# Sums of weight blocks in a seven-product matrix multiplication: two of four per head as VectorE additions, two as accumulating transfers, and the first rotary embeddings placed inside and behind head 0

## The chip, the core and the metric

The kernel runs on one core of a Trainium2 chip. The metric is the device time of one execution in microseconds, the median over several executions. A core has a matrix engine (TensorE, PE in the profile, with its weight loads as PEld), three engines for element-wise work (VectorE is DVE, ScalarE is ACT, GpSimd is POOL) and queues that start transfers: SP's hardware queue for plain loads, and POOL's software queue, the one used here for transfers that add to what lies in the target. Each engine works through its own instructions strictly in order, so an instruction that waits holds up all those behind it on its engine.

## The reference, cut to what matters

Two layers on a sequence of 512 rows with model width 1024. Layer 0 is a retention layer with four heads, layer 1 a forgetting attention with sixteen. The change lies in layer 0, in the projection from the modulated input `h` (512 x 1024) to queries, keys, values and gates:

```python
def _retention(h, positions, w_in, w_out):
    b, s, _ = h.shape
    n = s // CHUNK
    q, k, v, g = jnp.split(h @ w_in, [RET_DK, 2 * RET_DK, 2 * RET_DK + RET_DV], axis=-1)
    q = _rope(q.astype(jnp.float32).reshape(b, s, RET_HEADS, RET_HK), positions) * (RET_HK ** -0.5)
    k = _rope(k.astype(jnp.float32).reshape(b, s, RET_HEADS, RET_HK), positions)
...
    o = _layer_norm(_from_chunks(o)).reshape(b, s, RET_DV)
    return (o.astype(h.dtype) * jax.nn.silu(g)) @ w_out
```

For one head, values and gates together are `h @ [Wv | Wg]`, a product of 512 x 1024 by 1024 x 1024.

## The kernel before

**Precision.** Weights and activations are float32. Each matrix is split into a high and a low part of type fp32r (`split`: ACT casts the high part, DVE subtracts it to get the low part), and a product is three matrix instructions: high by high, high by low, low by high (`mm3`). Of a weight block, the loaded copy is `raw` (128 x 1024), its parts are `wh` (ACT) and `wl` (DVE).

**Seven products in place of eight.** `values_gates` computes a head's values and gates by the Strassen-Winograd form. The weight [Wv | Wg] is cut into four blocks: the upper and lower half of Wv (V1, V2) and of Wg (G1, G2), each loaded as two `raw` buffers of 512 KB. `h` is cut the same way, and sums of its quarters are prepared once (`forms[1]` to `forms[4]`, tiles `sf`). The products run in this order, each of 24 matrix instructions, in two halves of the inner dimension:

1. x = h11 by V1
2. y = h12 by V2
3. v = form 1 by (V1 + G1)
4. v += form 4 by G2
5. x += form 2 by (V1 + G1 + G2)
6. x += form 3 by (G1 + G2)
7. x += h22 by (V1 + G1 + G2 + V2)

Products 3, 5 and 7 use the buffers of V1 (`first`), to which one more block is added each time. Product 4 adds onto the banks of product 3, and products 5 to 7 onto those of product 1, so results that are needed as they are get copied out of PSUM first (`keep`, ACT, tile `u`): u5 between products 3 and 4, u2 between products 5 and 6. Between products 6 and 7, DVE subtracts x from u5 (`put_g(1, ...)`, tile `big`), and product 7 may write x only after that.

**The four sums before.** All four are accumulating transfers (`plus`): POOL issues a transfer of the block from DRAM that is added to the `raw` buffer in SBUF, two for a sum, eight for a head, 32 in all. Such a transfer can start only when the previous split of that buffer has been read (`wh` by ACT, `wl` by DVE), and the next split waits until it has landed.

**What sets the order.** The program is written as a list of tasks with priorities; `Sched.order` plays it through with assumed costs and buffer counts and so fixes, ahead of the run, the order of instructions on each engine. The assumed time of flight of an accumulating transfer comes from `t.bytes`, which `cost` multiplies by 2; at 360 KB per us and with two constants (0.6 and 1.4 us) this makes 4.9 us for 512 KB. `s.at(x)` shifts the priority of what is created inside it. Buffers `raw` (8), `wh` (4), `wl` (4) and `ck` share 14 places (N_B).

**Around it.** The first queries and keys (q of head 0, k of head 0, q of head 1) are computed in the start phase, copied out of PSUM (`kept`, tiles `rt`), and rotated later by `rope`: six DVE operations of 128 x 512, and four splits. All three ropes are created ahead of head 0 with a priority 25 us later (LATE). Heads 1 to 3 are merged with the retention of the head before (`merge`), whose matrix instructions (tile `r`) also fill gaps. The modulation weights (`in_mod_w`) are loaded along the way and multiplied into `macc` on DVE.

Of the kernel before, what the change touches and what calls it, by code (L numbers as in the profile page):

```python
# [10 lines left out]
ALU = mybir.AluOpType  # L11
# [6 lines left out]
D = 1024  # L18
# [16 lines left out]

ORD = "m0:2 q0:0 k0:0 m2:2 q1:0 m4:2 q0:1 k0:1 m6:2 q1:1"

DIRECT = 4

SUMS = -22.0  # L40

TRIG, DIFF = -12.0, 0.0

KEEP, LATE = -4.0, 25.0

GO = -6.0

# [128 lines left out]
class Sched:  # L176
# [63 lines left out]
    def cost(self, t, op, args, kw, ins, outs):  # L240

        n = max([v.words() for v in outs], default=0)
        if op == "dma_start":
            v = (ins + outs)[0]
            t.bytes = 4 * v.words() * (v.part[1] - v.part[0])
            if not outs:
                t.bytes = 4 * ins[0].words() * (ins[0].part[1] - ins[0].part[0])
            if "accum_op" in kw:
                t.bytes *= 2
            return {"POOL": 1.02, "SP": 0.06, "ACT": 0.1}[t.eng]  # L250
        if t.eng == "PE":
            if op == "transpose":
                t.cols = 256
                return 0.109
            m = args[2].words()
            t.cols = m if args[2].dtype == F32R else 4 * m
            if m < 64:
                return 0.213
            return max(0.109, 0.002 + m / 2260.0) if args[2].dtype == F32R else max(0.109, m / 600.0)
        ptr = sum(isinstance(kw.get(k), View) for k in ("scale", "bias", "scalar", "scalar1"))  # L260
        if t.eng == "ACT":
            if op == "activation" and args[2] in TABLES:
                t.table = TABLES[args[2]]
            sb = ins[0].buf.kind not in PSUM_KINDS
            return 0.052 + n / 1200.0 + 0.093 * (ptr + ("accum_out" in kw)) + 0.042 * sb
        if t.eng == "POOL":
            return 0.1 + n / (1050.0 if op == "tensor_scalar" else 450.0)
        n = max([n] + [v.words() for v in ins])
        psum = any(v.buf.kind in PSUM_KINDS for v in ins + outs)
        fast = op in ("tensor_scalar", "tensor_copy") and not psum  # L270
        return 0.069 + 0.061 * ptr + n / (1920.0 if fast else 960.0)
# [227 lines left out]
def run(gen):  # L499
    for _ in gen:  # L500
        pass
# [18 lines left out]
def trunk(tc, x, c, positions, mod_w, mod_b, norm_g, ret_w_in, ret_w_out, fox_w_in, fox_b_f,  # L520
# [6 lines left out]
    with ExitStack() as es:  # L527
# [6 lines left out]
        s = Sched(tc, KINDS, {"C": (N_C, slots), "B": (N_B, slots), "G": (4, slots), "T": (24, tiny), "Z": (8, psp)})  # L534
        V, A, G, T, SY = s.vector, s.scalar, s.gpsimd, s.tensor, s.sync
# [115 lines left out]
        class MItem:  # L651


            def __init__(self, layer, cols, rows, fin, prev):
                self.layer, self.cols, self.rows, self.fin, self.prev = layer, cols, rows, fin, prev
                self.n = sum(n for _, n in cols)
                self.direct = layer == 0 and cols[0][0] == 0 and rows[-1] < DIRECT

            def load(self):
                r = s.buf("raw", 1024)  # L660
# [110 lines left out]
        def rows2(src, col, i):  # L771
            return src[:, 2 * i:2 * i + 2, col:col + 512]

        def w_s(h):


            return [Block(rows2(wi0, col, i)) for col, lo in ((vcol(h), 0), (vcol(h), 2), (gcol(h), 2), (gcol(h), 0))
                    for i in (lo, lo + 1)]

        def w_b(src, col):  # L780
# [8 lines left out]
        def vcol(h):  # L789
            return 2048 + h * 512  # L790

        def gcol(h):
            return 4096 + h * 512
# [174 lines left out]
        def quarter(i, j):  # L968

            c = slice(256 * i, 256 * i + 256)  # L970
            return [(h[:, c], l[:, c]) for h, l in hT[4 * j:4 * j + 4]]
# [75 lines left out]
        def values_gates(h):  # L1047

            vc, gc = vcol(h), gcol(h)

            def heads(raw):

                def f(i):
                    hh, ll = s.buf("wh", 1024, F32R), s.buf("wl", 1024, F32R)
                    split(raw[i], hh, ll)
                    return [(hh[:, k * 512:k * 512 + 512], ll[:, k * 512:k * 512 + 512]) for k in range(2)]
                return f

            def whole(n):
                return [R(("vg", h, n), i) for i in range(2)]

            def plus(raw, col, lo):
                with s.at(SUMS):
                    for i in range(2):
                        G.dma_start(raw[i].rearrange("p (k n) -> p k n", k=2, n=512), rows2(wi0, col, lo + i),
                                    accum_op=ALU.add)
                return heads(raw)

            def product(banks, a, w, new):
                for kp in range(2):
                    with s.at(PROC):
                        ws = w(kp)
                    for tl in range(2):
                        if new and kp == 0:
                            banks.append(pt_())
                        ts = slice(tl * P, tl * P + P)
                        for k in range(2):
                            hh, ll = a()[2 * kp + k]  # L1080
                            mm3(banks[tl], hh[:, ts], ll[:, ts], *ws[k], new and kp + k == 0, kp == 1 and k == 1,
                                skip_group_check=True)
                            yield 0.683

            def keep(banks):
                us = [s.buf("u") for _ in range(2)]
                for u, b in zip(us, banks):
                    A.copy(u, b)
                return us

            put_v, put_g = values_out(h), gates_out(h)
            x, y, v = [], [], []
            first = whole(0)
            yield from product(x, lambda: quarter(0, 0), heads(first), True)
            u1 = keep(x)
            yield from product(y, lambda: quarter(0, 1), heads(whole(1)), True)
            put_v(0, y, u1)
            yield from product(v, lambda: forms[1], plus(first, gc, 0), True)
            u5 = keep(v)
            yield from product(v, lambda: forms[4], heads(whole(2)), False)  # L1100
            yield from product(x, lambda: forms[2], plus(first, gc, 2), False)
            u2 = keep(x)
            put_g(0, v, u2)
            yield from product(x, lambda: forms[3], plus(whole(3), gc, 2), False)
            put_g(1, u5, x)
            yield from product(x, lambda: quarter(1, 1), plus(first, vc, 2), False)
            put_v(1, x, None)
# [70 lines left out]
        kept = []  # L1178
        for b in start_banks:
            kept.append(s.buf("rt"))  # L1180
            with s.at(KEEP):
                A.copy(kept[-1], b)
        with s.at(LATE):
            for i, key in enumerate((("q", 0), ("k", 0), ("q", 1))):
                rope(key, kept[2 * i], kept[2 * i + 1])

        def head(h):
            if h > 1:
# [23 lines left out]
        mask = const("mask", [P])  # L1212
        gain = const("gain", [2])

        run(head(0))
        small_operands()
        for h in range(1, RH):
            merge(head(h), retention(h - 1), R0, B0, s)

# [428 lines left out]
```

## Time and profile before

| what | us |
|---|---|
| median of three runs | 751.24 (748.67 to 754.83) |
| the profiled execution, its own time | 749.46 |
| span of the profiled execution, first to last instruction | 747.7 |

The profiled execution lies 1.78 us under the median. The span is 1.76 us shorter than that execution's time. In the profile nearly all instructions carry one line of a helper, so groups are told apart by tile names: `wl<-raw,wh` is the DVE half of a weight split, `wh<-raw` the ACT half, `u<-p` a copy out of PSUM, `macc<-raw,...` the modulation sums, `p<-wh,sf` and `p<-wh,act` are matrix instructions of the seven products. In a timeline row, the bracket at the end gives how long the engine had been idle before this instruction, and what it waited for.

### The profile page before, as it was taken

Reading aid. Unit: us, or ns where it says so; the run is one execution under the profiler, and the core shown is the slowest. Engines: PE = TensorE matmul, PEld = TensorE weight load, DVE = VectorE, ACT = ScalarE, POOL = GpSimd, SP = SyncE. Lnnn points to the kernel's source line nnn. Section 1 sums busy time; section 2 is a strip of 40 time slices with the busy share of each in tenths; the row PEclk is TensorE's granted clock in tenths of the full one; section 3 lists DMA queues with packets and bytes.
Section 4 is the critical chain, followed back from the end, with each engine's and each line's share of the span. In section 5 each row is a group of like instructions: output and inputs, shape, how many; then the busy total and the mean of one; then the engine's idle time right before and its main releaser. Section 6 shows DMA issues by size and latency. Waiting matters only on the chain.

```text
span 747.7 us, 9994 instructions
## 1 busy us (share of the span) xinstructions
PE 711.4 (95%) x3386; PEld 583.0 (78%) x3386; DVE 586.9 (78%) x1289; ACT 395.8 (53%) x733; POOL 114.4 (15%) x135
## 2 busy tenths in 40 slices
PE   7999989989997999999999999889999999999995
PEld 6777868767886888788888887668887778888884
DVE  5889987769866878798753677868698889899925
ACT  6567563535254534464322453448585677778612
POOL 1002101110121012100000101142214223120011
PEclk9999999999999999999999999999999999999998
DMA  8996948975598649935343407446435344446302
GB/s 282 349 310 143 227 134 215 240 202 189 128 205 225 229 113 203 262 125 186 113 138 102 160 37 233 136 139 157 126 90 147 95 128 118 120 125 192 118 1 112
DMA packets 78434, 122.51 MB, mean 164 GB/s; under 512 B 6712, under 2 KB 35632, under 8 KB 78384
## 3 DMA queue, kind: packets, MB, share of 16 engines
q1 hardware_dynamic: 66320, 98.78, 40.7%
q0 software_dynamic: 12064, 23.10, 17.0%
q8 instruction: 26, 0.43, 0.2%
q14 instruction: 24, 0.20, 0.1%
HBM read 113.42 MB, written 4.25 MB: 157 GB/s over the span
## 4 chain that ended last, share of the span: by engine, by line
PE 42%; DVE 7%; issue 5%; ACT 2%; POOL 1%; DMA 1%; POOLq 0%; ACTq 0%; DVEq 0%
PE a L440 18%; PE p L440 16%; PE r L440 8%; DVE t L440 3%; DVE macc L440 1%; DVE wl L440 1%; DVE st L440 1%; ACT st L440 1%; DMA ck<-cum_dram 1%; POOL ck L440 1%; DVE z L440 0%; DVE lg L440 0%; POOL qn L440 0%; ACT tm L440 0%; DVE ph L440 0%
## 5 line engine op out<-in xcount | busy, mean ns | idle before, releaser
L440 DVE TENSOR_TENSOR wl<-raw,wh 128x1024 fp32r<-128x1024 f32 x120 | 146.3, 1225 | 37.3 <-ACT wh L440 32.3
L440 ACT CAST wh<-raw 128x1024 fp32r<-128x1024 f32 x120 | 125.0, 1053 | 84.3 <-PE p L440 19.7
L440 PE MATMUL p<-wh,big 128*128 128x512 f32 x384 | 136.2, 402 | 0.0
L440 PE MATMUL p<-wh,sf 128*128 128x512 f32 x256 | 82.6, 399 | 7.4 <-ACT u L440 7.4
L440 PEld LDWEIGHTS p<-wh,big 128*128 128x128 f32 x384 | 71.9, 188 | 13.2 <-issue 0.2
L440 POOL DMA_DIRECT2D raw<-in_ret_w_in x32 | 38.9, 1263 | 267.7 <-DVE wl L440 167.9
L440 PE MATMUL p<-wl,big 128*128 128x512 f32 x192 | 76.6, 399 | 0.0
L440 PE MATMUL p<-wh,act 128*128 128x512 f32 x192 | 63.8, 402 | 5.4 <-DVE big L440 5.4
L440 DVE SCALAR_TENSOR_TENSOR macc<-raw,csilu,macc 128x512 f32<-128x512 f32 x80 | 60.6, 757 | 4.8 <-DMA raw<-in_mod_w 3.8
L440 PEld LDWEIGHTS p<-wh,sf 128*128 128x128 f32 x256 | 48.8, 191 | 19.8 <-ACT u L440 9.7
L440 PE MATMUL a<-wh,go 128*128 128x512 f32 x192 | 62.0, 393 | 0.0
L440 PE MATMUL p<-act,wh 128*128 128x512 f32 x160 | 53.2, 393 | 0.0
L440 PE MATMUL p<-wl,sf 128*128 128x512 f32 x128 | 51.1, 399 | 1.0 <-DVE wl L440 1.0
L440 PE MATMUL p<-big,wh 128*128 128x512 f32 x128 | 48.0, 424 | 0.0
L440 PEld LDWEIGHTS p<-wh,act 128*128 128x128 f32 x192 | 36.6, 192 | 13.4 <-DVE big L440 6.0
L440 ACT ACTIVATE lg<-lg,t 128x128 f32<-128x128 f32 (+1 forms) x64 | 36.3, 567 | 16.2 <-DVE t L440 14.6
L440 PEld LDWEIGHTS a<-wh,go 128*128 128x128 f32 x192 | 36.1, 188 | 7.2
L440 PEld LDWEIGHTS p<-wl,big 128*128 128x128 f32 x192 | 36.2, 188 | 6.0
L440 PE MATMUL r<-act,sh 128*128 128x512 f32 x120 | 40.3, 391 | 0.0
L440 PE MATMUL p<-wl,act 128*128 128x512 f32 x96 | 38.7, 403 | 0.7 <-DVE wl L440 0.7
L440 PE MATMUL a<-wl,go 128*128 128x512 f32 x96 | 37.5, 391 | 0.0
L440 DVE TENSOR_TENSOR ph<-r,ph 128x512 fp32r<-128x512 f32 (+2 forms) x64 | 30.7, 485 | 5.4 <-ACT ph L440 5.0
(183 smaller groups left out, 1499.0 us busy)
## 6 DMA issues: line engine op xcount, KB each, us to landing
raw<-in_ret_w_in SPq DMA_DIRECT2D x48, 512.0 KB, 6.1
raw<-in_mod_w SPq DMA_DIRECT2D x64, 256.0 KB, 6.7
raw<-in_ret_w_in POOLq DMA_DIRECT2D x32, 512.0 KB, 7.6
raw<-in_fox_w_in SPq DMA_DIRECT2D x32, 512.0 KB, 3.9
raw<-in_mod_w SPq DMA_DIRECT2D x16, 512.0 KB, 6.5
raw<-in_ret_w_out SPq DMA_DIRECT2D x16, 512.0 KB, 4.4
ck<-cum_dram SPq DMA_DIRECT2D x16, 448.0 KB, 4.6
x<-in_x SPq DMA_DIRECT2D x16, 256.0 KB, 5.2
```

The lines of the kernel that those rows point to most:

```text
L440: getattr(eng, op)(*[real(v) for v in args], **{k: real(v) for k, v in kw.items()})
```

## The change

Two of the four sums become DVE additions. G1 and G2 are now loaded as blocks of their own (`block(2)`, `block(3)`); `sum2` adds G1 to V1's buffer before product 3 and G2 before product 5, on DVE, in place, 128 x 1024, just ahead of the split. The accumulating transfers that stay are G2 onto G1's buffer (product 6, `third`) and V2 onto V1's buffer (product 7). The number of loads through SP stays at eight per head; the list of blocks `w_s` now has G1 ahead of G2, since G1 is needed first.

The ropes move: q and k of head 0 are created after 24 steps of head 0 (a step is three matrix instructions, 24 steps are three products), q of head 1 after head 0, each with a priority of 4 us later in place of 25. The planner's `t.bytes` for an accumulating transfer is multiplied by 4 in place of 2, which makes its assumed flight 7.8 us. `DIRECT` becomes a tuple; its first entry is the old value and the others are 0, so the same items are direct as before.

```diff
-DIRECT = 4
+DIRECT = (4, 0, 0, 0)
...
-KEEP, LATE = -4.0, 25.0
+KEEP, LATE = -4.0, 4.0
+
+ROPE_AT = 24
...
             if "accum_op" in kw:
-                t.bytes *= 2
+                t.bytes *= 4
...
-                self.direct = layer == 0 and cols[0][0] == 0 and rows[-1] < DIRECT
+                self.direct = layer == 0 and cols[0][0] < D and rows[-1] < DIRECT[cols[0][0] // 256]
...
-            return [Block(rows2(wi0, col, i)) for col, lo in ((vcol(h), 0), (vcol(h), 2), (gcol(h), 2), (gcol(h), 0))
+            return [Block(rows2(wi0, col, i)) for col, lo in ((vcol(h), 0), (vcol(h), 2), (gcol(h), 0), (gcol(h), 2))
                     for i in (lo, lo + 1)]
...
-            first = whole(0)
+            def sum2(raw, other):
+
+                def f(i):
+                    V.tensor_tensor(out=raw[i], in0=raw[i], in1=other()[i], op=ALU.add)
+                    return heads(raw)(i)
+                return f
+
+            kept = {}
+
+            def block(n):
+                if n not in kept:
+                    kept[n] = whole(n)
+                return kept[n]
+
+            first = block(0)
...
-            yield from product(y, lambda: quarter(0, 1), heads(whole(1)), True)
+            yield from product(y, lambda: quarter(0, 1), heads(block(1)), True)
             put_v(0, y, u1)
-            yield from product(v, lambda: forms[1], plus(first, gc, 0), True)
+            yield from product(v, lambda: forms[1], sum2(first, lambda: block(2)), True)
+            third = plus(block(2), gc, 2)
             u5 = keep(v)
-            yield from product(v, lambda: forms[4], heads(whole(2)), False)
-            yield from product(x, lambda: forms[2], plus(first, gc, 2), False)
+            yield from product(v, lambda: forms[4], heads(block(3)), False)
+            yield from product(x, lambda: forms[2], sum2(first, lambda: block(3)), False)
             u2 = keep(x)
             put_g(0, v, u2)
-            yield from product(x, lambda: forms[3], plus(whole(3), gc, 2), False)
+            yield from product(x, lambda: forms[3], third, False)
             put_g(1, u5, x)
             yield from product(x, lambda: quarter(1, 1), plus(first, vc, 2), False)
...
-        with s.at(LATE):
-            for i, key in enumerate((("q", 0), ("k", 0), ("q", 1))):
+        def start_rope(i, key, late):
+            with s.at(late):
                 rope(key, kept[2 * i], kept[2 * i + 1])
...
-        run(head(0))
+        steps = head(0)
+        for _ in range(ROPE_AT):
+            next(steps)
+        for i, key in enumerate((("q", 0), ("k", 0))):
+            start_rope(i, key, LATE)
+        run(steps)
         small_operands()
+        start_rope(2, ("q", 1), LATE)
```

How the order of instructions moves is shown at three places. A number behind a name is that buffer's own; the two programs number buffers differently.

The first place is DVE in head 0 just ahead of product 2. `rt` are ropes, `sf` and `sx` the sums of quarters of `h`, `raw_512` is V2's first buffer, and in the changed program `raw_495` and `raw_506` are V1, `raw_535` and `raw_549` G1. Before:

```order
L440 TENSOR_TENSOR sx_727<-x_613,sx_727 128x256
L440 TENSOR_TENSOR rt_740<-rt_672,trig_725 128x512
L440 TENSOR_TENSOR rt_746<-rt_672,trig_707 128x512
L440 TENSOR_TENSOR rt_672<-rt_689,trig_707 128x512
L440 TENSOR_TENSOR wl_757<-raw_512,wh_744 128x1024
```

After:

```order
L442 TENSOR_TENSOR sx_731<-sx_721,x_451 128x256
L442 TENSOR_TENSOR raw_495<-raw_495,raw_535 128x1024
L442 TENSOR_TENSOR sx_731<-x_612,sx_731 128x256
L442 TENSOR_TENSOR raw_506<-raw_506,raw_549 128x1024
L442 TENSOR_TENSOR wl_760<-raw_512,wh_744 128x1024
```

Three rope operations have left the place ahead of product 2's first split, and two additions for product 3 stand there; one `sf` that stood behind that split (`sf_161`) also stands ahead of it now, some rows earlier (`sf_144`).

The second place is DVE at the end of head 0, around the hand-over from product 6 to product 7. `raw_495` and `raw_506` are V1's buffers with all blocks added, product 7's weights; the last two `big` rows of each list are the ones that product 7 must wait for. Before:

```order
L440 TENSOR_TENSOR wl_1021<-raw_495,wh_997 128x1024
L440 TENSOR_TENSOR act_1029<-rt_908,act_1017 128x512
L440 TENSOR_TENSOR big_1038<-p_826,u_992 128x512
L440 TENSOR_TENSOR act_1044<-rt_934,act_1033 128x512
L440 TENSOR_TENSOR big_1038<-p_838,u_1009 128x512
L440 TENSOR_TENSOR wl_1055<-raw_506,wh_1040 128x1024
L440 SCALAR_TENSOR_TENSOR act_1064<-vr_841,t_853,act_1048 128x512
L440 TENSOR_TENSOR big_1038<-u_863,p_710 128x512
L440 TENSOR_TENSOR big_1038<-u_881,p_722 128x512
```

After:

```order
L442 TENSOR_TENSOR wl_1001<-raw_495,wh_966 128x1024
L442 TENSOR_TENSOR act_1008<-rt_943,act_997 128x512
L442 TENSOR_TENSOR big_1014<-p_822,u_960 128x512
L442 TENSOR_TENSOR act_1022<-rt_962,act_1010 128x512
L442 TENSOR_TENSOR big_1014<-p_834,u_975 128x512
L442 TENSOR_TENSOR big_1014<-u_862,p_710 128x512
L442 TENSOR_TENSOR big_1014<-u_872,p_719 128x512
L442 TENSOR_TENSOR sf_1052<-r_1016,dec_805 128x512
L442 TENSOR_TENSOR sf_1059<-r_1027,dec_805 128x384
L442 TENSOR_TENSOR rt_1063<-rt_736,trig_723 128x512
L442 TENSOR_TENSOR wl_1069<-raw_506,wh_1055 128x1024
```

The split of product 7's second half (`wl_1055`, `wl_1069`) stood ahead of the two `big` rows and stands four rows behind them now; the rope of q of head 1 (`rt_1063` is its first row) begins here, where it ended before.

The third place is ACT in head 1 between products 5 and 7. `u` are the copies that product 6 waits for, `raw_988` before and `raw_950` after is V1's first buffer with all blocks added. Before:

```order
L440 CAST wh_1533<-raw_1307 128x1024
L440 CAST wh_1553<-raw_988 128x1024
L440 COPY u_1565<-p_1291 128x512
L440 COPY u_1577<-p_1303 128x512
L440 ACTIVATE big_1570<-big_1570 128x512 x2
L440 CAST wh_1593<-raw_1002 128x1024
```

After:

```order
L442 CAST wh_1530<-raw_1277 128x1024
L442 COPY u_1559<-p_1283 128x512
L442 COPY u_1572<-p_1298 128x512
L442 ACTIVATE big_1564<-big_1564 128x512 x2
L442 CAST wh_1588<-raw_950 128x1024
L442 ACTIVATE big_1564<-big_1564 128x512 x2
L442 CAST wh_1636<-raw_987 128x1024
```

The cast that needs the transfer of product 7's first half stood ahead of the two copies and stands behind them now.

## The prediction

> **What bounds the kernel now.** I read the page's busy times first, then its costly groups and transfers, then windows of the heads stage, then the timeline of PE for its stalls, and from each stall back to the engine that released it. From the page:
>
> ```profile
> span 747.7 us, 9994 instructions
> PE 711.4 (95%) x3386; PEld 583.0 (78%) x3386; DVE 586.9 (78%) x1289; ACT 395.8 (53%) x733; POOL 114.4 (15%) x135
> ...
> raw<-in_mod_w SPq DMA_DIRECT2D x64, 256.0 KB, 6.7
> ...
> raw<-in_ret_w_in POOLq DMA_DIRECT2D x32, 512.0 KB, 7.6
> ```
>
> PE is busy 95% of the span, so the number of matrix instructions sets the time, and the change alters none of them. Only PE's idle time and its clock can move. A transfer that adds 512 KB takes 7.6 us from issue to landing. The change touches the four heads, 62 to 345 us. In the windows, the columns are window, length, then busy time of PE, PEld, DVE, ACT, POOL, the granted clock of PE, the share of the transfer engines, GB/s:
>
> ```profile
> 62.00:345.00 283.00, 268.52 (x1216) 220.26 (x1215) 232.47 (x437) 141.40 (x223) 37.61 (x31) 0.99 0.74 188
> 60.00:96.00 36.00, 35.27 (x156) 28.54 (x156) 35.93 (x57) 23.96 (x36) 8.54 (x7) 1.00 0.94 208
> 104.00:108.00 4.00, 4.00 (x13) 3.14 (x12) 4.00 (x6) 2.70 (x4) 0.00 (x0) 0.60 0.00 0
> 172.00:176.00 4.00, 4.00 (x20) 3.30 (x19) 3.93 (x7) 2.34 (x5) 0.00 (x0) 1.00 0.18 52
> 228.00:232.00 4.00, 2.54 (x7) 2.04 (x8) 3.87 (x5) 2.90 (x4) 0.53 (x1) 0.76 0.75 242
> 232.00:236.00 4.00, 4.00 (x16) 3.15 (x15) 2.23 (x3) 1.49 (x2) 1.91 (x2) 0.81 0.64 94
> ```
>
> In the heads PE idles 283.00 − 268.52 = 14.5 us, and DVE 50.5. The lowered clock costs (1 − 0.60) × 4 = 1.6 us at 104 to 108, and 0.24 × 2.54 + 0.19 × 4 = 1.4 us at 228 to 236. So the most that the change can gain is 14.5 + 1.6 + 1.4 = 17.5 us. PE's stalls there, in its timeline, add up to the same 14.5:
>
> ```profile
> 69.11 0.50 PE L440 MATMUL p<-wl,act 128*128 128x512 f32 x1 [0.73 <-DVE wl L440]
> ...
> 102.38 0.50 PE L440 MATMUL p<-wh,act 128*128 128x512 f32 x1 [2.74 <-DVE big L440]
> ...
> 145.79 0.50 PE L440 MATMUL p<-wh,sf 128*128 128x512 f32 x1 [0.88 <-ACT u L440]
> ...
> 155.81 0.50 PE L440 MATMUL p<-wl,sf 128*128 128x512 f32 x1 [0.96 <-DVE wl L440]
> ...
> 159.99 0.50 PE L440 MATMUL p<-wh,sf 128*128 128x512 f32 x1 [1.40 <-ACT u L440]
> ...
> 169.72 0.50 PE L440 MATMUL p<-wh,act 128*128 128x512 f32 x1 [2.62 <-DVE big L440]
> ...
> 229.46 0.50 PE L440 MATMUL p<-wh,sf 128*128 128x512 f32 x1 [3.76 <-ACT u L440]
> ...
> 314.88 0.50 PE L440 MATMUL p<-wh,sf 128*128 128x512 f32 x1 [1.40 <-ACT u L440]
> ```
>
> The 1.6 us follow the stall at 102.38, the 1.4 us the one at 229.46.
>
> **Part 1: sixteen additions on DVE.** The trace has no 128x1024 addition. The nearest rows are three splits in a row, and an addition in place of half that size:
>
> ```profile
> 88.56 3.50 DVE L440 TENSOR_TENSOR wl<-raw,wh 128x1024 fp32r<-128x1024 f32 x3
> 91.97 0.69 DVE L440 TENSOR_TENSOR act<-rt,act 128x512 fp32r<-128x512 f32 x1
> ...
> L440 DVE TENSOR_TENSOR raw<-raw,gate x48: 660/685/693, 313.2 to 709.4; 128x512 f32<-128x512 f32 x48
> ```
>
> By the first, an addition occupies 3.41 / 3 = 1.14 us (88.56 to 91.97), by the second at most 2 × 0.685 = 1.37. I take 1.14, the same shape: 16 × 1.14 = 18.2 us (21.9 at most), and DVE in the heads goes from 232.5 to 250.7 of 283 us. What hides them is DVE's 50.5 idle us; without that cover they cost up to 18.2. On DVE the splits queue behind an addition, and PE waits for those. Against that, sixteen accumulating transfers (8.4 MB) go, and with them sixteen waits of DVE and ACT for a landing. SP's loads stay eight a head; the sums now wait for a plain load, issued ahead, instead of a transfer that cannot start before the old split is read. POOL's queue issues 16 instead of 32, `third` ahead of V2's pair; at 1.2 us a row of the 37.6 that POOL is busy, this costs nothing, as nothing but these transfers waits for POOL. `DIRECT` changes nothing, and the planner's 7.8 us change only the order.
>
> **Part 2: head 0.** Product 2 waits for a split behind three rope operations:
>
> ```profile
> 65.91 2.01 DVE L440 TENSOR_TENSOR rt<-rt,trig 128x512 f32<-128x512 f32 x3
> 67.84 1.22 DVE L440 TENSOR_TENSOR wl<-raw,wh 128x1024 fp32r<-128x1024 f32 x1
> ```
>
> They take 67.84 − 65.91 = 1.93 us, 0.64 each. In their place stand two additions and one `sf` (0.64): 2.28 + 0.64 − 1.93 = 1.0 us later, since DVE has no idle time here (35.93 of 36 us, 60 to 96). Loss 1.0, the stall at 69.11 becomes 1.7. The moved rope operations of head 0 end at the same row as before (the splits ahead of the first `big`), and only the retention merged with head 1 reads them: no wait.
>
> Product 7 waits for DVE to free its banks (`big`), and DVE stands in front of a split of the second V2 sum:
>
> ```profile
> 90.23 1.23 POOL L440 DMA_DIRECT2D raw<-in_ret_w_in  x1 [3.08 <-DVE wl L440]
> 98.75 1.05 ACT L440 CAST wh<-raw 128x1024 fp32r<-128x1024 f32 x1 [3.50 <-DMA raw<-in_ret_w_in]
> 99.84 1.23 DVE L440 TENSOR_TENSOR wl<-raw,wh 128x1024 fp32r<-128x1024 f32 x1 [1.83 <-ACT wh L440]
> 101.64 1.28 DVE L440 TENSOR_TENSOR big<-u,p 128x512 f32<-128x512 f32 x2
> ```
>
> The transfer, issued at 90.23, lands 8.5 us later, and the wait passes through ACT and DVE to PE. In the new order the two `big` rows stand ahead of the split. Up to them DVE has 4 × 1.14 = 4.6 us of additions more, and the rope of q of head 1 less (six operations and two splits at 0.64 = 5.1), so it comes no later than before, 0.5 us earlier. Before, its queue ahead of the waiting split ended at 99.84 − 1.83 = 98.0. So `big` starts near 98, product 7 about 0.7 us behind it (101.64 to 102.38), at 98.7, where PE still has other work to 102.38 − 2.74 = 99.64. The stall of 2.74 goes, with the 1.6 us of clock behind it. Late next is product 7's second half, whose weights are now split behind two `big`, two `sf` and a rope operation: 5 × 0.64 = 3.2 us, to 101.2, and then 1.14, to 102.4. Its first half, 12 instructions at 268.52 / 1216 = 0.22 us, ends at 99.64 + 2.65 = 102.3 and the first matrix instructions of a half need only the high part; I put 0.5 us there (0 to 2.6, a half product). Head 0: 2.74 + 1.6 − 1.0 − 0.5 = +2.8.
>
> **Part 3: head 1.** Its last three stalls have the landing of V2's transfers behind them:
>
> ```profile
> 158.40 1.05 ACT L440 CAST wh<-raw 128x1024 fp32r<-128x1024 f32 x1 [2.66 <-DMA raw<-in_ret_w_in]
> 159.36 1.07 ACT L440 COPY u<-p 128x512 f32<-128x512 f32 x2
> ...
> 165.62 2.00 ACT L440 CAST wh<-raw 128x1024 fp32r<-128x1024 f32 x2 [2.56 <-DMA raw<-in_ret_w_in]
> ...
> 168.98 1.28 DVE L440 TENSOR_TENSOR big<-u,p 128x512 f32<-128x512 f32 x2
> ```
>
> At 158.40 ACT waits 2.66 us with the copies for product 6 behind it; the new order has the copies first, which ends the stall of 1.40. At 165.62 the same wait as in head 0 delays `big`; the planner, reckoning with 7.8 us of flight, now keeps that split back. I let 4.4 of 0.88 + 0.96 + 1.40 + 2.62 = 5.9 go and keep 1.5, since DVE here has additions and the rope of q of head 1 (5.1) more.
>
> **Part 4: heads 2 and 3.** The largest stall hangs on modulation weights:
>
> ```profile
> 210.85 3.70 POOL L440 DMA_DIRECT2D raw<-in_ret_w_in  x3 [8.80 <-DMA raw<-in_ret_w_in]
> 218.43 0.99 SPq L440 DMA_DIRECT2D raw<-in_mod_w  x2
> 226.57 0.49 DVE L440 TENSOR_SCALAR macc<-raw,csilu 128x512 f32<-128x512 f32 x1 [5.76 <-DMA raw<-in_mod_w]
> 227.88 1.05 ACT L440 CAST wh<-raw 128x1024 fp32r<-128x1024 f32 x1 [4.27 <-DVE macc L440]
> 228.83 0.58 ACT L440 COPY u<-p 128x512 f32<-128x512 f32 x1
> ```
>
> DVE waits for a load issued at 218.43 that lands 8 us later (median 6.7), while accumulating transfers issued from 210.85 on still move; ACT waits 4.27 us for DVE and the copy behind it holds product 4. With half of those transfers gone the load lands sooner: I let 4.0 of 3.76 + 1.4 (clock) go (0 to 5.2). For head 3's 1.40 I take nothing.
>
> **New waits.** In heads 1 to 3, twelve additions (13.7 us) can wait for their loads, and stand ahead of splits. Bounds are 0 and 18.2. How DVE's waits reach PE, the waits view of the heads shows:
>
> ```profile
> DVE macc L440 <- DMA raw<-in_mod_w: 16.1, 5, 5.8
> ```
>
> Of these 16.1 us, PE lost 3.76 + 0.88, as most stood in gaps. I take 2.0, nearest to that: about three in ten (4.64 / 16.1) of 7 us, half of the additions' 13.7.
>
> **Sum.** 2.8 + 4.4 + 4.0 + 0 − 2.0 = 9.2 us, so this execution would take 749.46 − 9.2 = 740.3. The median stands 1.78 above it: 742.0.
>
> **Rivals.** *The waits only move.* The transfer onto V1 for product 7 is still there, in two of eight places as late as before, and DVE comes to `macc` at another time but still waits. Then only 0.88 + 0.96 + 1.40 = 3.2 go and 1.0 + 2.0 are lost: 749.46 − 0.2 + 1.78 = 751 (748 without the new losses, 754 without the gain). For it: DVE waits in five places for `in_mod_w` and PE felt only two, so a shift of DVE's order can bring out others.  Against it: the order at both product 7s has changed.
>
> *DVE becomes the bound (slower).* In head 0 it has no idle time from 60 to 96 already. In heads 1 to 3, if its 16.1 us for `in_mod_w` and its waits for ACT's halves stay whole, the additions push the splits behind them, and PE waits for `wl`: up to 749.46 + 18.2 + 1.78 = 769 if the other parts gain nothing, and 749.46 − 11.2 + 18.2 + 1.78 = 758 if they gain their 2.8 + 4.4 + 4.0. It decides from the point where the additions push PE's splits by 7.5 us more than the other parts gain. For it: DVE waits now for ACT's halves as well as for loads, and an addition stands ahead of the very split it feeds. Against it: 250.7 is still 32 us short of 283. [...]
>
> *Nearly all goes.* All 17.5 but the 1.0 and 0.5 of head 0: 749.46 − 16.0 + 1.78 = 735.2. For it: behind most of the eight stalls stands a DVE or ACT wait for a transfer, and the change reorders those.
>
> *The clock's dip is not tied to the stall.* After 2.74 us of idling the clock was 0.60, after 2.62 (169.72) it was 1.00 at 172 to 176. If the dip comes from elsewhere, 1.6 stays lost: 742.0 + 1.6 = 743.6. [...]
>
> **How the numbers follow.** Forecast 0.45 (its own range 738 to 747: 742.0 less the 2.0 of new waits and the rest of the clock and wait in head 2, 1.2, at the low end, plus head 1's 4.4 at the high end), waits move 0.24, DVE bound 0.14, nearly all 0.12, clock 0.05. A measurement can tell about 1% here, 7.5 us: below 743.7 is faster, above 758.8 slower. Faster: 0.6 of the forecast's chance (0.27), 0.12, and 0.03 of the clock's: 0.42. Slower: most of DVE bound, 0.12. The rest, 0.46, is within 1%. The range 735 to 754 leaves out DVE bound (0.14) and half of nearly-all (0.06).
>
> **What would show it.** Right: no stall over 1 us at product 7 of heads 0 and 1; the clock at 1.00 behind it; the copies of head 1 without a stall; a wait for `in_mod_w` in head 2 under 3 us; DVE busy up by about 18, sixteen accumulating transfers; PE idle in the heads near 7 and product 2's stall near 1.7. Wrong: DVE's additions waiting for loads with PE waiting for `wl` behind them, or DVE without idle time beyond head 0.

## The result, and the profile after

| | before | after |
|---|---|---|
| median, us | 752.14 (748.67 to 754.83, 4 runs) | 731.63 (731.38 to 733.41, 4 runs) |
| ratio after / before, 95% interval | | 0.9735 (0.969 to 0.9779) |
| profiled execution, us | 749.46 | 731.40 |

The change makes the kernel 2.65% faster, about 20 us. The forecast was 742.0 with a range from 735 to 754: the direction was right, the size about half of what came, and the time lies 3.4 us under the range. (The median before is of four runs here; the page ahead gave 751.24 for the first three of them.)

The page of the changed kernel, the same lines as before, and its row for the accumulating transfers:

```profile
span 729.6 us, 9987 instructions
PE 708.0 (97%) x3386; PEld 581.5 (80%) x3386; DVE 603.7 (83%) x1305; ACT 394.8 (54%) x733; POOL 94.8 (13%) x119
...
raw<-in_ret_w_in POOLq DMA_DIRECT2D x16, 512.0 KB, 8.8
```

PE's instructions are the same 3386; DVE has sixteen more, POOL sixteen less. The transfers that are left take longer to land (8.8 us in place of 7.6), so they have not become cheap; fewer things wait for them.

Where the 18.1 us of span went is seen when both programs are cut at the same instructions: the last matrix instruction of the start phase (62.1 us before, 62.0 after) and the last `a<-wl,go` of the output projection (409.7 and 391.6). What follows takes 338.0 us in both. So all of the gain lies between. The windows of that stage, first before, then after (columns as in the prediction):

```profile
62.10:409.70 347.60, 333.12 (x1517) 273.94 (x1516) 271.88 (x502) 162.29 (x251) 37.61 (x31) 0.99 0.69 181
```

```profile
62.00:391.60 329.60, 327.86 (x1516) 271.83 (x1515) 287.08 (x515) 161.78 (x251) 19.45 (x16) 1.00 0.59 167
```

Idle time of PE fell from 14.5 to 1.7 us, by 12.7. But its busy time fell as well, by 5.3 us, with the same instructions. Part of that is the clock: before, two stretches of 3.4 us ran at half of it, each right behind one of the long stalls, 3.4 us lost in all. Before:

```profile
103.80:107.20 3.40, 3.40 (x10) 2.63 (x9) 3.40 (x6) 2.31 (x4) 0.00 (x0) 0.50 0.00 0
...
230.10:233.50 3.40, 3.40 (x10) 2.62 (x9) 3.37 (x4) 2.29 (x3) 1.22 (x1) 0.50 0.25 68
```

The other 1.9 us are near what each stall costs beside its idle time. In a stream a matrix instruction begins every 0.23 us and is recorded 0.39 us long (62.33 and 62.56 before), so the last one ahead of a stall counts as busy for 0.16 us more than its share. The first one behind a stall is recorded 0.50 us long, and the next begins 0.34 us after it (69.11 and 69.45 before), which is 0.11 more. Six stalls fewer at 0.27 make 1.6; this is worked out, not measured by itself.

All the stalls that PE has left in the heads, in its timeline after the change:

```profile
68.74 0.50 PE L442 MATMUL p<-wl,act 128*128 128x512 f32 x1 [0.50 <-DVE wl L442]
...
229.67 0.47 PE L442 MATMUL p<-wh,act 128*128 128x512 f32 x1 [1.24 <-DVE big L442]
```

Eight stalls have become two. ACT's waits for a weight block to land (62 to 345 us) had been these before, and after the change its list has none:

```profile
ACT wh L440 <- DMA raw<-in_ret_w_in: 14.6, 7, 4.1
```

DVE's waits there: before, 16.1 us for `in_mod_w` in five places; after:

```profile
DVE wl L442 <- ACT wh L442: 4.6, 7, 1.1
DVE big L442 <- ACT u L442: 4.1, 3, 2.6
DVE macc L442 <- DMA raw<-in_mod_w: 2.0, 1, 2.0
```

No line says that an addition waits for its load. And DVE without any idle time did not hold PE up here: from 84 to 100 us, the place of product 5 to product 7 of head 0, both are busy all the time.

```profile
84.00:100.00 16.00, 16.00 (x74) 13.20 (x73) 16.00 (x25) 8.10 (x12) 1.22 (x1) 1.00 0.83 226
```

### The profile page after: what moved, and what is told of

It is laid out like the page before. It is cut to its first block, busy times and chain, and to the rows that moved or that the text cites. A ratio compares the mean times of both kernels' runs of the same rounds, so it can differ in the third digit from the quotient of the medians.

```text
span 729.6 us, 9987 instructions
## 1 busy us (share of the span) xinstructions
PE 708.0 (97%) x3386; PEld 581.5 (80%) x3386; DVE 603.7 (83%) x1305; ACT 394.8 (54%) x733; POOL 94.8 (13%) x119
## 3 DMA queue, kind: packets, MB, share of 16 engines
q0 software_dynamic: 7712, 14.71, 10.5%
## 4 chain that ended last, share of the span: by engine, by line
PE 76%; DVE 9%; issue 6%; DMA 5%; ACT 2%; POOL 1%; SPq 1%; DVEq 0%; POOLq 0%; ACTq 0%
PE p L442 42%; PE a L442 18%; PE r L442 13%; DVE t L442 3%; DMA raw<-in_mod_w 3%; PE s L442 2%; DVE macc L442 2%; DVE wl L442 2%; DMA raw<-in_ret_w_in 1%; DVE st L442 1%; ACT st L442 1%; DMA ck<-cum_dram 1%; SPq L442 1%; POOL ck L442 1%; DVE z L442 0%
## 5 line engine op out<-in xcount | busy, mean ns | idle before, releaser
L442 PE MATMUL p<-wh,sf 128*128 128x512 f32 x256 | 79.7, 390 | 0.0
L442 PE MATMUL a<-wh,go 128*128 128x512 f32 x192 | 62.1, 394 | 0.0
L442 POOL DMA_DIRECT2D raw<-in_ret_w_in x16 | 19.5, 1242 | 268.0 <-DVE raw L442 87.7
```

Source lines behind the costliest of these rows:

```text
L442: getattr(eng, op)(*[real(v) for v in args], **{k: real(v) for k, v in kw.items()})
```

## The experiments

The change has three parts: the sums, the ropes and the planner's flight. Each can be in or out by itself, which makes eight kernels with the two that are known. The other six were run, then five that vary one quantity in the changed kernel, and one that divides the ropes. The edits are cut to what matters; the `DIRECT` tuple of the change came along in all of them, and it changes nothing.

**flight_only.** The kernel before with the planner's figure alone.

```diff
             if "accum_op" in kw:
-                t.bytes *= 2
+                t.bytes *= 4
```

> The kernel before with one edit: the planner reckons 7.8 us of flight for an accumulating transfer in place of 4.9. All four sums stay transfers and the ropes stay where they were. If the order of instructions is what the change gains by (theory O), the casts and splits that wait for a landing stand later, the stalls of 2.74, 2.62 and 1.40 us go and the time is 744 or less. If it is the number of transfers that must land inside a head (theory L), the same 32 waits stay, PE stalls elsewhere instead, and the time is 748 to 754.

Measured: 757.69 us, ratio 1.0075 (1.0051 to 1.0099), slower than either theory said. The profiled execution took 753.06, the fastest of nine; the other eight had a granted clock of 0.978 to 0.986 in place of its 0.987, so part of what the median has more is clock that this profile doesn't show. In the profile PE idles 14.8 us in the stage, as long as before, although ACT waits for no weight block there any more. The planner believes 32 transfers to be slow, moves matrix instructions of the retention ahead of products whose operands were late, and these then wait in their place (the first row). PE's timeline:

```profile
90.52 0.50 PE L442 MATMUL r<-act,sh 128*128 128x512 f32 x1 [1.89 <-ACT act L442]
...
149.16 0.50 PE L442 MATMUL p<-wh,sf 128*128 128x512 f32 x1 [3.40 <-ACT u L442]
```

The second has DVE's wait for `in_mod_w` behind it (3.83 us, DVE's timeline), as the largest stall before had:

```profile
146.27 0.49 DVE L442 TENSOR_SCALAR macc<-raw,csilu 128x512 f32<-128x512 f32 x1 [3.83 <-DMA raw<-in_mod_w]
```

**ropes_only.** The kernel before with the ropes moved.

```diff
-KEEP, LATE = -4.0, 25.0
+KEEP, LATE = -4.0, 4.0
...
-        run(head(0))
+        steps = head(0)
+        for _ in range(ROPE_AT):
+            next(steps)
+        for i, key in enumerate((("q", 0), ("k", 0))):
+            start_rope(i, key, LATE)
+        run(steps)
         small_operands()
+        start_rope(2, ("q", 1), LATE)
```

> The kernel before with the ropes alone moved (q and k of head 0 after three products, q of head 1 after head 0). Theory R (the ropes are what delays DVE in head 0): the stall of 0.73 us at product 2 goes, and one bank row of product 7 is freed ahead of the waiting split, so 2.74 us and the 1.6 us of clock go too: about 746. Theory L: the landing of the second V2 sum still holds the other bank, the heads 1 to 3 are as before: 748 to 754.

Measured: 749.11 us, ratio 0.9968 (0.9939 to 0.9996), in the range of theory L. Head 0 is repaired, as theory R said: of the stalls at 69.11 and 102.38 nothing is left. But the heads behind it stall 10.8 us in all, as before (11.0), and in other places. The clock takes about half of the gain again: PE idles 3.5 us less in the stage (11.0 in place of 14.5) but is busy 1.9 us longer (334.97 in place of 333.12). The mean granted clock is 0.98 there in place of 0.99, and behind these stalls matrix instructions begin 0.42 to 0.43 us apart in place of 0.23, from 150.42 to 155.09, from 226.77 to 230.17 and from 312.69 to 315.25. PE's timeline:

```profile
149.83 0.80 PE L442 MATMUL p<-wl,sf 128*128 128x512 f32 x1 [3.27 <-DVE wl L442]
...
225.49 0.50 PE L442 MATMUL p<-wh,sf 128*128 128x512 f32 x1 [3.85 <-ACT u L442]
...
312.09 0.80 PE L442 MATMUL p<-wh,sf 128*128 128x512 f32 x1 [2.59 <-ACT u L442]
```

**sums_only.** The kernel before with `sum2` for products 3 and 5, and the blocks loaded as in the change.

```diff
-            yield from product(v, lambda: forms[1], plus(first, gc, 0), True)
+            yield from product(v, lambda: forms[1], sum2(first, lambda: block(2)), True)
...
-            yield from product(x, lambda: forms[2], plus(first, gc, 2), False)
+            yield from product(x, lambda: forms[2], sum2(first, lambda: block(3)), False)
```

> The kernel before with two of four sums per head on DVE alone; planner's flight 4.9 us, ropes all ahead of head 0. Theory L: the waits for in_mod_w and for the sums of products 3 and 5 shrink with half of the accumulating transfers gone, the two stalls at product 7 stay in part since the split of V2's sum stands ahead of the two big rows: 735 to 740. Theory O: without the planner's new figure the stalls stay: 746 or more. If DVE becomes the bound with ropes and additions both in head 0 (theory D): PE waits for wl in head 0 and the time is 750 or more.

Measured: 742.23 us, ratio 0.987 (0.9836 to 0.9904), between the theories and nearest to L. The waits for `in_mod_w` fall to 3.2 us and the stalls of 3.76 and 1.40 us in heads 2 and 3 go or shrink with them. Theory D holds in one place: with ropes and additions both in head 0, DVE comes to the last `big` rows at 105.74, 4 us later than before. PE's timeline, then DVE's:

```profile
105.22 0.50 PE L442 MATMUL p<-act,wl 128*128 128x512 f32 x1 [3.52 <-DVE wl L442]
```

```profile
102.69 2.48 DVE L442 TENSOR_TENSOR wl<-raw,wh 128x1024 fp32r<-128x1024 f32 x2
105.08 0.74 DVE L442 SCALAR_TENSOR_TENSOR act<-vr,t,act 128x512 fp32r<-128x512 f32 x1
105.74 1.28 DVE L442 TENSOR_TENSOR big<-u,p 128x512 f32<-128x512 f32 x2
```

**sums_as_before.** The changed kernel with all four sums as accumulating transfers.

```diff
-            yield from product(v, lambda: forms[1], sum2(first, lambda: block(2)), True)
+            yield from product(v, lambda: forms[1], plus(first, gc, 0), True)
...
-            third = plus(block(2), gc, 2)
...
-            yield from product(x, lambda: forms[3], third, False)
+            yield from product(x, lambda: forms[3], plus(whole(3), gc, 2), False)
```

> The changed kernel with the four sums as accumulating transfers again; the ropes moved and the planner's flight 7.8 us, as changed. Theory L: nearly the whole gain is gone, 746 to 754. Theory O or R: most of it stays, 740 or less.

Measured: 752.94 us, ratio 1.0033 (1.0012 to 1.0054). The whole gain is gone, as theory L said: without the sums the two other edits are worth nothing.

**flight_as_before.** The changed kernel with the planner's old figure.

```diff
-                t.bytes *= 4
+                t.bytes *= 2
```

> The changed kernel with the planner's flight 4.9 us again. Theory L: the sums carry the gain, the splits of V2's sum stand ahead of big again at product 7 of heads 0 and 1, so up to 2 x 2.7 us of stall can come back: 732 to 738. Theory O: 742 or more.

Measured: 738.09 us, ratio 0.9841 (0.9791 to 0.989), at the upper end of theory L and short of O. The landing of V2's sum shows again in head 1. ACT's timeline, then PE's:

```profile
159.25 2.94 ACT L442 CAST wh<-raw 128x1024 fp32r<-128x1024 f32 x3 [3.58 <-DMA raw<-in_ret_w_in]
```

```profile
161.30 0.73 PE L442 MATMUL p<-act,wh 128*128 128x512 f32 x2 [1.88 <-ACT wh L442]
```

One row stands for three casts, so the first, which waited 3.58 us, held up those behind it, and PE needed one of these.

**ropes_as_before.** The changed kernel with all ropes created ahead of head 0.

```diff
-KEEP, LATE = -4.0, 4.0
+KEEP, LATE = -4.0, 25.0
...
-        steps = head(0)
...
-        run(steps)
+        run(head(0))
         small_operands()
-        start_rope(2, ("q", 1), LATE)
```

> The changed kernel with all three ropes created ahead of head 0 again, 25 us later in priority. Theory L: within 2 us of the changed kernel, unless the split of V2's sum, which stands ahead of the last two big rows in head 0, waits for its landing (2.7 us and 1.6 us of clock): 732 to 737. Theory D: additions and ropes together overfill DVE in head 0, PE waits for wl or big there, 740 or more.

Measured: 742.58 us, ratio 0.9891 (0.9841 to 0.9942): theory D, not L. ACT waits for no transfer here, so landing is not the cause. DVE works at ropes with no gap in front of the last `big` rows. DVE's timeline, then PE's:

```profile
90.29 3.09 DVE L442 TENSOR_TENSOR rt<-rt,trig 128x512 f32<-128x512 f32 x5
93.30 1.28 DVE L442 TENSOR_TENSOR rt<-rt,rt 128x512 f32<-128x512 f32 x2
...
103.46 1.27 DVE L442 TENSOR_TENSOR big<-u,p 128x512 f32<-128x512 f32 x2
```

```profile
104.19 0.79 PE L442 MATMUL p<-wh,act 128*128 128x512 f32 x1 [2.86 <-DVE big L442]
...
165.62 0.47 PE L442 MATMUL p<-wh,act 128*128 128x512 f32 x1 [2.41 <-DVE big L442]
```

**q1_rope_ahead.** The changed kernel with the rope of q of head 1 alone created ahead of head 0.

```diff
+        start_rope(2, ("q", 1), 25.0)
         steps = head(0)
...
-        start_rope(2, ("q", 1), LATE)
```

> The changed kernel with the rope of q of head 1 created ahead of head 0 again (25 us later in priority); the ropes of q and k of head 0 stay in the middle of head 0. Its eight operations (5.1 us) are back on DVE between product 5 and the last big rows of head 0, beside the 4.6 us of additions. If that queue is what the move relieves, big comes 4 to 5 us later, PE stalls 2 to 4 us at product 7 of head 0 and loses up to 1.7 us of clock: 734 to 738. If the gain of the moved ropes (11 us with the two other edits in place) hangs on the order of the later heads, which the planner changes as a whole, product 7 of head 0 stalls less than 1 us and the time shows no fixed amount.

Measured: 740.14 us, ratio 0.9868 (0.9831 to 0.9905). The last `big` rows move from 97.66 in the changed kernel to 105.14, 7.5 us later, and PE stalls 3.12 and 0.96 us there, the longer time for `act`, a split of a rope in the same queue of DVE. It is the queue of head 0, more than forecast. DVE's row in the changed kernel, then here, then PE's:

```profile
97.66 1.27 DVE L442 TENSOR_TENSOR big<-u,p 128x512 f32<-128x512 f32 x2
```

```profile
105.14 1.28 DVE L442 TENSOR_TENSOR big<-u,p 128x512 f32<-128x512 f32 x2
```

```profile
98.24 0.91 PE L442 MATMUL r<-act,act 128*128 128x512 f32 x3 [0.96 <-ACT act L442]
...
102.27 2.59 PE L442 MATMUL r<-act,act 128*128 128x512 f32 x8 [3.12 <-DVE act L442]
```

**spare_transfers.** The changed kernel with sixteen transfers more that nobody reads.

```diff
+                    for i in range(2):
+                        G.dma_start(spare_dram.pop().rearrange("p (k n) -> p k n", k=2, n=512), rows2(wi0, col, lo + i))
```

> The changed kernel with sixteen transfers of 512 KB more on POOL's queue, from the same weights to scratch DRAM, spread over the four heads, read by nobody; the order on PE, DVE, ACT and SP is the changed kernel's, row for row. If the gain came from the traffic that went (sixteen transfers less, contention for in_mod_w and the other loads), most of the 9 us that the sums brought return: 738 to 742, with DVE waiting for in_mod_w again. If it came from nobody having to wait for those sixteen to land, the time stays within 2 us of the changed kernel's 731.6.

Measured: 734.88 us (733.59 to 735.56), ratio 0.9784 (0.9758 to 0.981): 3.3 us more than the changed kernel, between the two, nearer to the second. In the profiled executions the stage of the heads is 2.1 us longer and what follows it 1.6 us, for a reason that the last section shows. DVE's wait for `in_mod_w` is 2.5 us, the longest 1.9 (2.0 in the changed kernel; 16.1 and 5.8 before), so this traffic does not bring the long wait back. One stall is new, and it has a plain load behind it that came late. DVE's timeline, then PE's:

```profile
302.81 1.29 DVE L446 TENSOR_TENSOR raw<-raw,gate 128x512 f32<-128x512 f32 x2 [1.38 <-DMA raw<-in_ret_w_out]
304.03 1.28 DVE L446 TENSOR_TENSOR big<-u,p 128x512 f32<-128x512 f32 x2
```

```profile
304.76 0.51 PE L446 MATMUL p<-wh,act 128*128 128x512 f32 x1 [1.64 <-DVE big L446]
```

So traffic costs something, about 2 us here, but not the 9 us that the sums bring. These transfers write to DRAM and don't add in SBUF; whether the latter burdens the queues more was not tried.

**sums_three.** A third sum on DVE.

```diff
-            third = plus(block(2), gc, 2)
+            third = sum2(block(2), lambda: block(3))
```

> The changed kernel with a third sum on DVE (G2 onto G1, product 6), so that only V2's pair goes by accumulating transfer: 8 additions or 9.1 us more on DVE, 248.2 to 257 of the 267 us of the heads. If DVE's fullness costs little as long as it has some idle time, 730 to 733, since PE has only 1.7 us of stalls left to lose there. If DVE is near the point where it bounds, PE waits for wl and the time is 735 to 741.

Measured: 735.34 us, ratio 0.9795 (0.9756 to 0.9835), 3.7 us more than with two, and at the low end of the second range.

**sums_doubled.** Each addition made twice, so that the products use V1 + 2 G1 and so on; only its time is of use.

```diff
                     V.tensor_tensor(out=raw[i], in0=raw[i], in1=other()[i], op=ALU.add)
+                    V.tensor_tensor(out=raw[i], in0=raw[i], in1=other()[i], op=ALU.add)
```

> The changed kernel with each of the sixteen additions made twice (the products then use V1 + 2 G1 and so on), which puts 18.2 us more on DVE, 248.2 to 266.4 of the 267 us of the heads; the planner knows it. If DVE is the bound from there on, as the rival of the prediction has it, the heads can't hold it: PE waits for wl or big by 8 us or more, 740 or more. If DVE's work can be moved out of the heads by the planner, or its waits shrink instead, 735 or less.

Measured: 741.17 us, ratio 0.9873 (0.9841 to 0.9904). In the changed kernel the 18.2 us of additions leave PE no more than 1.7 us of stalls; 18.2 more cost 9.5, and 9.1 more (with eight transfers less) cost 3.7. PE idles 5.6 us in the stage, less than the 8 expected; two lowered stretches of the clock, one of them behind the heads, cost 1.5 (eight matrix instructions in the 3.38 us from 96.96 to 100.34, in a stream 0.23 each) and 1.4 (a row at 469.57 of 3.74 us, 2.33 in the changed kernel). The stalls that came are where DVE had been full already, in head 0. PE's timeline of sums_doubled and DVE's share there:

```profile
96.15 0.50 PE L442 MATMUL p<-wl,sf 128*128 128x512 f32 x1 [2.11 <-DVE wl L442]
```

```profile
76.00:98.00 22.00, 18.14 (x73) 13.46 (x72) 21.97 (x31) 13.14 (x18) 3.63 (x3) 0.98 0.70 156
```

**flight_x3** and **flight_x6.** The changed kernel with another figure for the planner; the second has 6 in the place of 3.

```diff
-                t.bytes *= 4
+                t.bytes *= 3
```

> The changed kernel with the planner's flight at 6.4 us (factor 3). If the figure has to reach what the transfers really take (8.8 us median in the changed kernel), part of the 6.5 us between 4.9 and 7.8 us comes back: 733 to 737. If any order behind the first works, 732.

> The changed kernel with the planner's flight at 10.7 us (factor 6). If the figure only has to be large enough, within 2 us of 731.6. If too large a figure makes the planner put other work ahead of what is ready, as it did with four transfers a head (757.7), 735 or more.

Measured: 735.16 us (734.4 to 736.62), ratio 0.9792 (0.9765 to 0.982), and 737.53 us (737.22 to 738.13), ratio 0.9822 (0.9797 to 0.9847): a figure below the measured flight gives part of the gain, and one above it costs again. With 4.9, 6.4, 7.8 and 10.7 us of assumed flight the times are 738.1, 735.2, 731.6 and 737.5 (the stage alone, in the profiled executions: 336.5, 331.4, 329.6 and 333.8). The best is near the measured 8.8 us, but four points don't show that this is why: the planner changes the whole order with each.

The eight combinations together, as ratios to the kernel before:

| | old ropes, 4.9 us | new ropes, 4.9 us | old ropes, 7.8 us | new ropes, 7.8 us |
|---|---|---|---|---|
| four transfers | 1 | 0.9968 | 1.0075 | 1.0033 |
| two additions, two transfers | 0.987 | 0.9841 | 0.9891 | 0.9735 |

One at a time, the three edits make −1.3, −0.3 and +0.75%, which adds up to −0.85%; together they make −2.65%. Of the kernels run, none is faster than the changed one.

In the profiled executions, PE's idle time in the stage and ACT's waits for a weight block to land, in us:

| | old ropes, 4.9 us | new ropes, 4.9 us | old ropes, 7.8 us | new ropes, 7.8 us |
|---|---|---|---|---|
| four transfers | 14.5; 14.6 | 11.0; 15.2 | 14.8; none | 14.1; none |
| two additions, two transfers | 8.3; 6.6 | 5.4; 11.6 | 7.8; none | 1.7; none |

The planner's 7.8 us end ACT's waits in all four kernels that have them. With four transfers PE gains nothing by it: the rows of flight_only show instructions that were moved to the front and wait there themselves. With two transfers and the ropes moved, 5.4 us become 1.7. So a wait that is gone from the list need not be time won.

## Why the prediction was wrong in size

The places were right: PE's stalls in the heads behind landings and behind DVE's queue, and the clock with them. The step that failed is the term "New waits", −2.0, together with the stalls that the sum kept: it let PE idle near 7 us in the heads, and 1.7 are left. Each was a guess between bounds. And the sum drew 7.2 us (2.8 + 4.4) from the order of rows in heads 0 and 1, which it put down to the ropes and the planner's figure, and outside head 2 it counted the additions as a cost to be hidden; the runs show the additions as the condition, since the two other edits gain nothing without them (sums_as_before) and the sums alone gain 9.3 us (sums_only). The rival that *nearly all goes* (735.2, chance 0.12) describes the trace. The steps one by one, each against the trace of the changed kernel (us of gain that the forecast missed):

- **New waits, 2.0 taken, none found: 2.0.** No addition waits for a load; in the one run where one does (1.5 us in head 1 of q1_rope_ahead), PE does not stall behind it. DVE's additions, 18.2 us by their price, went into idle time that it had spent waiting for `in_mod_w` (16.1 us, now 2.0) and for ACT's halves (13.6, now 4.6), and the planner knew of them. The price of 1.14 us was right; DVE's timeline:

```profile
64.86 1.22 DVE L442 TENSOR_TENSOR raw<-raw,raw 128x1024 f32<-128x1024 f32 x1
66.00 0.42 DVE L442 TENSOR_TENSOR sx<-x,sx 128x256 f32<-128x256 f32 x1
```

- **Product 2, 1.0 lost by forecast, 0.2 gained: 1.2.** The stall went from 0.73 to 0.50. The two additions took 2.28 us as reckoned. But a `tg` row and the `sf` had moved further up, ahead of the split at 62.72, which came no later than before (62.69), so between that split and product 2's there was less work: 4.75 us in place of 5.15. The prediction counted the `sf` as new work and began its reckoning one split too late.
- **Product 7 of head 0, 0.5 kept for its second half: 0.5.** The last `big` rows were forecast near 98 and began at 97.66. The stall of 2.74 and the slow clock are gone, and so is the half-product's wait.
- **Head 1, 1.5 kept of 5.9: 1.5.** All of it went.
- **Head 2, 4.0 taken of 5.2.** The stall of 3.76 and its clock went, and one of 1.24 came at product 7, behind a shorter wait for `in_mod_w`. The size was right, in part by luck: the load that ended DVE's wait before was not the one issued at 218.43 but one issued at 215.68, which landed at 226.55 after 10.9 us, and spare_transfers does not show that half of the traffic gone is why its counterpart took 7.8. DVE's timeline:

```profile
226.37 0.75 DVE L442 SCALAR_TENSOR_TENSOR macc<-raw,csilu,macc 128x512 f32<-128x512 f32 x1 [2.03 <-DMA raw<-in_mod_w]
```

- **Head 3, nothing taken of 1.40: 1.4.** It went too; sums_only shows that the sums alone nearly end it (0.30 is left there, and 0.69 comes at product 7).
- **The ceiling of 17.5.** It counted 1.6 + 1.4 us of clock where 3.4 were lost (0.4; at 230 the lowered stretch lay wholly in busy time), and left out what a stall costs PE beside its idle time (1.9). The stage gave back 18.0.
- **The median 1.78 above the profiled execution.** After the change it stands 0.23 above: 1.6. Before, the runs spread over 6 us, after it over 2. This fits a kernel in which transfers no longer reach PE, but no run was made on it.

These add up to 10.5 us, beside the 10.4 between 742.0 and 731.63.

Of the rivals, *the waits only move* is what the two smaller edits do without the sums (flight_only, sums_as_before and, behind head 0, ropes_only). *DVE becomes the bound* did not happen at sixteen additions, but it is close: sums_only and ropes_as_before show it in head 0, where the place of the ropes decides, and sums_doubled shows its slope. A DVE without idle time cost PE nothing in the changed kernel from 84 to 100 us (DVE 16.00 of 16 us busy, PE 16.00), and held it up in sums_doubled from 76 to 98 (DVE 21.97 of 22, PE 18.14). That the clock's dip is tied to the stall holds for the dips at 104 and 230: they went with their stalls. Where the wait of 2.62, which brought none, differs from them is in the last section.

What stays open: why 7.8 us of assumed flight beats both 6.4 and 10.7, and how the 13 us that only the combination brings divide between waits and order. The runs show that the ropes give DVE room at product 7 of head 0 and the planner's figure takes casts out of the way of other casts in head 1; the rest lies in an order that differs in hundreds of rows.

## What to carry to other kernels

- An accumulating transfer that must wait for its target to be read, and whose landing the next step needs, put its flight in front of that step here: 7.6 us by the median from issue to landing, with 14.6 us of waits on ACT in the heads, the longest 4.1. An addition of 1.14 us on an engine with idle time, from a block loaded ahead, took its place. Here that was the condition for everything else.
- Edits on one queue were not additive here: with additions and ropes both on DVE in head 0, PE stalled 3.52 us (sums_only) and 2.86 us (ropes_as_before) there; with the ropes moved its one stall there was 0.50. Run the combinations before judging an edit by itself.
- When stalls are the bound, write down three prices for each: the idle time, the clock behind it (1.7 us here after the stalls of 2.74 and 3.76) and the restart (0.27 us, as worked out above). And let a stall go from the sum unless a row says what replaces it.

## What the runs showed of the hardware

The same wait of 2.60 us, later in the program (`r<-tm,z`, PE's timeline), is followed by full clock in the changed kernel (1.00 from 460.90 to 467.70) and by a lower one in q1_rope_ahead, where the same eight instructions take 3.92 us in place of 2.33:

```profile
462.26 2.33 PE L442 MATMUL r<-tm,z 128*16 128x512 f32 x8 [2.60 <-DVE z L442]
```

```profile
468.38 3.92 PE L442 MATMUL r<-tm,z 128*16 128x512 f32 x8 [2.60 <-DVE z L442]
```

Six of the kernels above are about 2 us slower behind the heads (about 340 us there in place of 338) with not one instruction changed or moved, and in all six this row is the long one: 3.74 to 4.02 us, which makes 1.4 to 1.7 of it. That is part of the 8.5 us of q1_rope_ahead and of the 9.5 of sums_doubled, for example. So a wait of 2.60 us came ahead of a lower clock in one position and not in another.

The traces show the position. In the profiles of the two kernels the lowered stretches (clock 0.50) begin whole multiples of 3.413 us apart (before: at 11.65, 21.89, 103.81 and 230.11, steps of 3, 24 and 37; after: at 20.59 and 723.73, a step of 206). Cut into windows by that grid, the wait of 2.60 us lies across two windows in the changed kernel (1.24 us idle in 457.49 to 460.90, 1.36 in the next). In q1_rope_ahead the clock is 0.87 from 100 to 104 us and 0.70 from 104 to 108, which puts its lowered stretch at about 102.98 to 106.40; by a grid from there the wait lies nearly whole in one window (2.43 us idle in 464.80 to 468.21). In the kernel before, the wait of 2.74 put 1.98 us into one window (100.40 to 103.81), the one of 3.76 put 2.77 (226.70 to 230.11), and the one of 2.62 put 1.57 and 1.05 into two. From 60 to 700 us of these two profiles, the clock was low behind the two windows in which PE idled 1.98 and 2.77 us, and behind none of the others, where it idled 1.57 us at most. That is two windows in two profiles; where between 1.57 and 1.98 us the difference lies, and whether idle time is all that counts, they don't show.
